# A two-layer decoder trunk: where the norms' squares are summed, and which engine splits one block of key weights

## The chip, the cores and the metric

One core of a Trainium2 chip runs the kernel. The metric is the device time of one execution in microseconds (us). The engines are TensorE (PE, the matmuls), VectorE (DVE), ScalarE (ACT), GpSimd (POOL), and SyncE (SP), whose queue issues the weight DMAs.

## What is computed

A trunk of two pre-norm residual layers on x of shape (1, 256, 1024), float32: an attention mixer, then a gated FFN with a causal depthwise convolution of width 3, and a last norm at the end. The first layer's mixer has two kinds of heads (one with a top-k selection), the second layer's a mixture of three dilated windows. Cut to what matters here:

```
def rmsnorm(x, g):
    y = x32 * lax.rsqrt(jnp.mean(x32 * x32, axis=-1, keepdims=True) + RMS_EPS)
    return (y * g.astype(jnp.float32)).astype(x.dtype)
...
def conv_ffn(h, w_up, conv_w, conv_b, w_down):
    u = h @ w_up
    ...
    val, gate = jnp.split(c, 2, axis=-1)
    return (jax.nn.silu(gate) * val) @ w_down
...
    for layer in range(DEPTH):
        h = rmsnorm(x, attn_norm[layer])
        ...
        x = x + mixed @ w_o[layer]
        h = rmsnorm(x, ffn_norm[layer])
        x = x + conv_ffn(h, w_up[layer], conv_w[layer], conv_b[layer], w_down[layer])
    return rmsnorm(x, final_norm)
```

## The kernel before

**Precision and weights.** Every large product is three matmuls, high x high, high x low and low x high (`mm3`, L125). An operand is split into a high part, which ACT copies into a rounded format (L121), and a low part, which DVE makes by subtraction (L122). Weights come in tiles of 1 MB by SP's queue (`load_cols` L90, `load_rows` L98). The tiles of the up projection and of q, k, v share three raw slots; five slots each hold the high and low parts. A load into a raw slot is issued when the last split that reads the slot's old contents is done. Names read as f0 (first FFN), f1 (second FFN), n1 (the norm ahead of the second layer's attention), q10, k10, v10 (first column block of that attention's projections), a0, a1 (the two attentions). f0w3_1h is the high part of the second weight block (the gate half, from the raw tile ug2) of up tile f=3; f0w3_0h is that of the value half (from uv2). Two consecutive f share a pair of raw tiles: uv0, ug0 serve f=0 and 1, uv2, ug2 serve f=2 and 3, uv4, ug4 serve f=4 and 5.

**The norms.** The residual x is kept transposed as xT, 8 blocks of 128 features by 256 tokens, and the products are formed from x times gain; the factor 1/sqrt(mean square) of each token is applied later, where a product leaves PSUM. `Norm.take` (L214) is called for each of four PSUM accumulators b: DVE adds it to xT (L219), ACT squares the result (L227), ACT and DVE make high and low parts, xh and xl (L203, L204). POOL adds the squares up as they come (L229, L231, L233: two of 128x512, three of 128x256 in each norm). After b = 3 PE sums over partitions ("sp", L239), DVE makes the mean ("v", L176), POOL the power -1/2 ("r", L178), DVE splits it and puts it on diagonals ("rh", "rl", "d", L183 to L190), PE broadcasts it to a row ("bp", L191), and ACT copies the row to SBUF ("b", L194). The sums and the broadcast use the PSUM bank called av.

**The FFN.** `ffn` (L470) runs over 22 tiles f. An up tile is 48 matmuls. Its PSUM banks rotate, `rot = [lg_tile, pt_tile, lg_tile, av_tile]`, so that f=3 is the first to use the bank av. DVE multiplies the tile by the scale row (us, L516), ACT and DVE do the convolution and the gate, ACT and DVE split the gated tile (g, L530 and L533), and three tiles later PE does its down product into the four accumulators f0o0 to f0o3. At the end of the first FFN the last tile's down products (g21) feed `take` of n1.

**The order.** No engine reorders at run time: each runs its own list. The list is set when the kernel is built, by a scheduler that simulates a timeline and takes, on each engine, what is ready and of the highest priority. The code narrows it: `tc.high_priority()` raises what stands in it, `keep_in_program_order` pins, and `issue_after(i)` (in `behind`, L107) keeps an instruction behind i. `n1.gate` are the last xh and xl of n1; weights split behind them don't come in their way. In the second attention (L751) the first half of the first key weights is split ahead of that gate, its low part on POOL:

```
        gate, low = (n1.gate, nc.gpsimd) if c == 0 else (None, nc.vector)
        proj_fm(wo1, 256 * c, n1.xh, n1.xl, q_evac(qs, rb1, f"q1{c}t"), f"q1{c}")
        proj_fm(wo1, 1024 + 256 * c, n1.xh, n1.xl, k_evac(ks, kl, rb1, f"k1{c}t"), f"k1{c}",
                (None, gate), (low, nc.vector))
```

Of the kernel before, what the change touches and what calls it, by code (L numbers as in the profile page):

```python
# [34 lines left out]
def trunk(ctx, tc, x, w_in_even, idx_k_norm, w_in_odd, w_o, rel_bias, attn_norm, ffn_norm,  # L35
          w_up, conv_w, conv_b, w_down, final_norm, c_onehot, out):
    nc = tc.nc
    cp = ctx.enter_context(tc.tile_pool(name="cp", bufs=1))
    wp = ctx.enter_context(tc.tile_pool(name="wp", bufs=2))
    tp = ctx.enter_context(tc.tile_pool(name="tp", bufs=2))  # L40
# [7 lines left out]
    def lg_tile(name):  # L48
        return pb.tile([P, 512], F32, tag="lg", name=name, bufs=2)
# [21 lines left out]
    ones = cp.tile([P, P], F32, tag="ones", name="ones")  # L71
# [39 lines left out]
                es.enter_context(tc.issue_after(i.ins))  # L111
            yield

    def split(view, shape, name, gate=None, low=nc.vector):
        with behind(gate):
            return split_now(view, shape, name, low)

    def split_now(view, shape, name, low):
        h = wp.tile([P] + shape, F32R, tag="wh", name=name + "h", bufs=5)
        l = wp.tile([P] + shape, F32R, tag="wl", name=name + "l", bufs=5)  # L120
        nc.scalar.activation(h, view, AF.Copy)  # L121
        low.tensor_tensor(l, view, h.bitcast(F32), ALU.subtract)  # L122
        return h, l

    def mm3(ps, wh, wl, ah, al, start, stop, swap=False, pin=False, **kw):  # L125
# [75 lines left out]
    def split_x(xh, xl, grow, k):  # L201
        g = gT[:, grow + k:grow + k + 1]
        a = nc.scalar.activation(xh[:, k, :], xT[:, k, :], AF.Copy, scale=g)  # L203
        v = nc.vector.scalar_tensor_tensor(xl[:, k, :], xT[:, k, :], g, xh[:, k, :].bitcast(F32),  # L204
                                           op0=ALU.mult, op1=ALU.subtract)
        return a, v

    class Norm:


        def __init__(self, grow, name):
            self.grow, self.name = grow, name

        def take(self, b, acc):  # L214
            if b == 0:
                self.xh, self.xl = norm_tiles(self.name)
            xv = xT[:, 2 * b:2 * b + 2, :]
            for i in range(2):
                nc.vector.tensor_tensor(xv[:, i, :], acc[:, i * S:(i + 1) * S], xv[:, i, :], ALU.add)  # L219
            with tc.high_priority():  # L220
                self.measure(b, xv)
            for k in (2 * b, 2 * b + 1):
                self.gate = split_x(self.xh, self.xl, self.grow, k)

        def measure(self, b, xv):
            sq = tp.tile([P, 2, S], F32, tag=("c", "c", "u", "c")[b], name=f"{self.name}sq{b}", bufs=(3, 3, 2, 3)[b])
            nc.scalar.activation(sq, xv, AF.Square)  # L227
            if b in (1, 2):
                nc.gpsimd.tensor_tensor(sq, sq, self.sq, ALU.add)  # L229
            if b >= 2:  # L230
                nc.gpsimd.tensor_tensor(sq[:, 0, :], sq[:, 0, :], sq[:, 1, :], ALU.add)  # L231
            if b == 3:
                nc.gpsimd.tensor_tensor(sq[:, 0, :], sq[:, 0, :], self.sq[:, 0, :], ALU.add)  # L233
            self.sq = sq
            if b < 3:
                return
            ps = av_tile(self.name + "sp")
            for t in range(2):
                nc.tensor.matmul(ps[:, t:t + 1], sq[:, 0, t * P:(t + 1) * P], ones[:, 0:1], start=True, stop=True)  # L239
            self.r = rsqrt_mean(ps[:, 0:2], D, self.name)  # L240
            self.rb = row_bcast(self.r, self.name)


    pin = tc.keep_in_program_order
    we = w_in_even[0]
    kiw_raw = cp.tile([P, 8, 80], F32, tag="kT", name="kiw_raw")
    nc.sync.dma_start(kiw_raw, we[:, 4096:4176].rearrange("(k p) c -> p k c", p=P))
# [18 lines left out]
    for b in range(4):  # L266
        h, l = (w[:, 2 * (b % 2):2 * (b % 2) + 2, :] for w in qi0_hl[b // 2])
# [6 lines left out]
        if b > 0:  # L274
            high = pin(nc.scalar.activation(h, wv, AF.Copy))
# [11 lines left out]

    def proj_fm(w2d, c0, xh, xl, evac, name, gate=(None, None), low=(nc.vector, nc.vector)):  # L290
        raw = load_cols(w2d, c0, name)
        ps = acc_tile(f"{name}p")
        for i in range(2):
            h, l = split(raw[:, :, i * P:(i + 1) * P], [8, P], f"{name}_{i}", gate[i], low[i])
            for k in range(KT):
                m = mm3(ps[:, i * S:(i + 1) * S], h[:, k, :], l[:, k, :], xh[:, k, :], xl[:, k, :],
                    k == 0 and i == 0, k == KT - 1, skip_group_check=True)
        evac(ps.rearrange("p (i c) -> p i c", i=2))
        return m
# [170 lines left out]
    def ffn(layer, norm, name, nxt, also=None):  # L470
        xh, xl = norm.xh, norm.xl
# [34 lines left out]
        for f in range(NF):  # L506
            if f % 2 == 0:
                raws = (load_cols(w_up[layer], f * P, f"{name}uv{f}"),
                        load_cols(w_up[layer], DFF + f * P, f"{name}ug{f}"))
            else:  # L510
                raw_dn = load_rows(w_down[layer], (f - 1) * P, f"{name}dn{f}", ("qT", "kT", "V")[f // 2 % 3])
                for i in range(2):
                    dn.append(raw_dn[:, i, :])
            ps = up(f, raws)
            u = tp.tile([P, 2, S], F32, tag="u", name=f"{name}us{f}")
            nc.vector.tensor_tensor(u, ps.rearrange("p (i c) -> p i c", i=2), rbb, ALU.mult)  # L516
            c = tp.tile([P, 2, S], F32, tag="c", name=f"{name}c{f}", bufs=3)
            for i in (1, 0):
                col = layer * 44 + i * NF + f
                nc.scalar.activation(c[:, i, :], u[:, i, :], AF.Identity, bias=cv[:, 3, col:col + 1],  # L520
                                     scale=cv[:, 2, col:col + 1])
                for j, sh in ((1, 1), (0, 2)):
                    nc.vector.scalar_tensor_tensor(c[:, i, sh:S], u[:, i, 0:S - sh], cv[:, j, col:col + 1],  # L523
                                                   c[:, i, sh:S], op0=ALU.mult, op1=ALU.add)
            sg = tp.tile([P, S], F32, tag="sg", name=f"{name}sg{f}")
            nc.scalar.activation(sg, c[:, 1, :], AF.Silu)
            nc.vector.tensor_tensor(sg, sg, c[:, 0, :], ALU.mult)
            g2 = tp.tile([P, 2, S], F32R, tag="g2", name=f"{name}g{f}", bufs=LAG + 2)
            gh, gl = g2[:, 0, :], g2[:, 1, :]
            high = nc.scalar.activation(gh, sg, AF.Copy)  # L530
            if also is not None:
                also(f, high.ins)
            nc.vector.tensor_tensor(gl, sg, gh.bitcast(F32), ALU.subtract)  # L533
            pend.append((f, gh, gl))
            if len(pend) > LAG:
                down(*pend.pop(0), dn.pop(0))
            if f == 1 and last:
                xtok = cp.tile([P, 2, D], F32, tag="qi", name=f"{name}xtok")
                for t in range(2):
                    for k4 in range(2):  # L540
                        px = acc_tile(f"{name}xt{t}{k4}")
                        for k in range(4):
                            nc.tensor.transpose(px[:, k * P:(k + 1) * P], xT[:, 4 * k4 + k, t * P:(t + 1) * P], ident)
                        nc.vector.tensor_copy(xtok[:, t, k4 * 512:(k4 + 1) * 512], px)
        if not last:
            down(*pend.pop(0), dn.pop(0))
        hl = [split(dn.pop(0), [D], f"{name}d{p[0]}") for p in pend]
        if not last:
# [205 lines left out]
    V, mxh, mxl = attn_tiles("a1")  # L754
    for c in range(4):
        qs, ks, kl = qk_tiles(c, "a1")
        gate, low = (n1.gate, nc.gpsimd) if c == 0 else (None, nc.vector)
        proj_fm(wo1, 256 * c, n1.xh, n1.xl, q_evac(qs, rb1, f"q1{c}t"), f"q1{c}")
        proj_fm(wo1, 1024 + 256 * c, n1.xh, n1.xl, k_evac(ks, kl, rb1, f"k1{c}t"), f"k1{c}",
                (None, gate), (low, nc.vector))  # L760
        proj_v(wo1, 2048 + 256 * c, n1.xh, n1.xl, r1, 256 * c, f"v1{c}", gate)
        for hp in (2 * c, 2 * c + 1):
            head_pair(hp, qs, ks, kl, lambda h: (nb1[:, h, P:S], nb1[:, h, :]), "a1")
# [45 lines left out]
```

## Time and profile before

| | us |
|---|---|
| median of 3 runs | 663.67 (663.56 to 664.44) |
| the profiled execution | 663.93 |
| its span on the core | 662.1 |
| PE busy | 649.3 (98%) |
| DVE busy | 530.5 (80%) |
| ACT busy | 406.2 (61%) |
| POOL busy | 58.0 (9%) |

The span runs from the first instruction to the last one on the core; the execution is 1.8 us longer. A share of busy time is a mean over stages: the first FFN runs from about 160 to 350 us of the span, the second layer's attention from there to 467, the second FFN to the end. Matmuls overlap, so the durations of single ones add up to more than the time in which they run; the distance of two starts tells what one costs.

### The profile page before, as it was taken

The numbers are of one execution on the slowest core, as the hardware profiler recorded it, in microseconds if no ns is written. First come the engines' busy times: TensorE is split into PE (matmuls) and PEld (weight loads), VectorE is DVE, ScalarE is ACT, GpSimd is POOL, SyncE is SP. The second block draws the span as 40 slices with busy tenths as digits, with TensorE's granted clock in tenths as the row PEclk, the third lists the DMA queues.
The fourth block names the chain that finished last, engine by engine and source line by source line (L and its number), as shares of the span: only waits on it lengthen the run. The fifth ranks groups of instructions, "written<-read, shape, count | busy, mean of one in ns | idle before, by whom it ended". The sixth has DMA issues, their size and how long they took to land.

```text
span 662.1 us, 12930 instructions
## 1 busy us (share of the span) xinstructions
PE 649.3 (98%) x5145; PEld 616.6 (93%) x5145; DVE 530.5 (80%) x1012; ACT 406.2 (61%) x710; POOL 58.0 (9%) x68
## 2 busy tenths in 40 slices
PE   8999999999999999999999999999999999999995
PEld 6999998988999999999989988999999999999994
DVE  5999998966898777777779977765999777777774
ACT  6766774765676555555546866764587555555553
POOL 0100001712100000000013111010300000000002
PEclk9999999999999999999999999999999999999998
DMA  9986644462766666666323534537366555555201
GB/s 272 292 243 188 174 137 153 157 220 98 247 216 207 208 207 207 207 207 207 128 65 128 192 101 155 191 128 256 117 184 227 195 186 185 184 185 187 105 1 63
DMA packets 91604, 116.01 MB, mean 175 GB/s; under 512 B 3447, under 2 KB 83191, under 8 KB 91544
## 3 DMA queue, kind: packets, MB, share of 16 engines
q1 hardware_dynamic: 86492, 110.09, 50.5%
q10 hardware_dynamic: 5052, 5.10, 3.3%
q8 instruction: 40, 0.66, 0.4%
q14 instruction: 20, 0.16, 0.1%
HBM read 113.35 MB, written 1.84 MB: 174 GB/s over the span
## 4 chain that ended last, share of the span: by engine, by line
PE 95%; DVE 2%; DMA 1%; issue 1%; SPq 0%; ACT 0%; POOL 0%; POOLq 0%; DVEq 0%
PE f0u L130 18%; PE f1u L130 18%; PE f1o L130 9%; PE f0o L130 9%; PE a0o L130 3%; PE a1o L130 3%; PE a0av L392 1%; PE a1av L392 1%; PE a_0pt L385 1%; PE v02p L130 1%; PE v11p L130 1%; PE v01p L130 1%; PE v12p L130 1%; PE v03p L130 1%; PE v13p L130 1%; PE k02p L130 1%
## 5 line engine op out<-in xcount | busy, mean ns | idle before, releaser
L130 PE MATMUL f0u<-f0xl,f0w_0h 128*128 128x256 f32 x176 | 49.5, 281 | 1.2 <-DVE f0xl L204 1.2
L130 PE MATMUL f1u<-f1xl,f1w_0h 128*128 128x256 f32 x176 | 49.5, 281 | 0.3
L130 PE MATMUL f0u<-f0xh,f0w_0l 128*128 128x256 f32 x176 | 49.2, 280 | 0.0
L130 PE MATMUL f1u<-f1xh,f1w_1h 128*128 128x256 f32 x176 | 49.2, 280 | 0.0
L130 PE MATMUL f0u<-f0xh,f0w_1l 128*128 128x256 f32 x176 | 49.1, 279 | 0.0
L130 PE MATMUL f1u<-f1xl,f1w_1h 128*128 128x256 f32 x176 | 49.1, 279 | 0.0
L130 PE MATMUL f1u<-f1xh,f1w_0l 128*128 128x256 f32 x176 | 49.1, 279 | 0.0
L130 PE MATMUL f0u<-f0xh,f0w_1h 128*128 128x256 f32 x176 | 49.1, 279 | 0.0
L130 PE MATMUL f0u<-f0xh,f0w_0h 128*128 128x256 f32 x176 | 49.1, 279 | 0.0
L130 PE MATMUL f0u<-f0xl,f0w_1h 128*128 128x256 f32 x176 | 49.1, 279 | 0.0
L130 PE MATMUL f1u<-f1xh,f1w_1l 128*128 128x256 f32 x176 | 49.1, 279 | 0.0
L130 PE MATMUL f1u<-f1xh,f1w_0h 128*128 128x256 f32 x176 | 49.1, 279 | 0.0
L523 DVE SCALAR_TENSOR_TENSOR f1c<-f1us,cv,f1c 128x255 f32<-128x255 f32 (+1 forms) x88 | 37.0, 475 | 0.7 <-ACT f1c L520 0.7
L523 DVE SCALAR_TENSOR_TENSOR f0c<-f0us,cv,f0c 128x255 f32<-128x255 f32 (+1 forms) x88 | 36.9, 476 | 0.0
L121 ACT ACTIVATE f1w_0h<-f1uv 128x1024 fp32r<-128x1024 f32 x22 | 23.2, 1056 | 21.9 <-PE f1u L130 21.9
L121 ACT ACTIVATE f0w_0h<-f0uv 128x1024 fp32r<-128x1024 f32 x22 | 23.3, 1057 | 21.8 <-PE f0u L130 21.5
L130 PEld LDWEIGHTS f0u<-f0xl,f0w_0h 128*128 128x128 f32 x176 | 33.1, 188 | 1.8 <-DVE f0xl L204 1.6
L130 PEld LDWEIGHTS f1u<-f1xl,f1w_0h 128*128 128x128 f32 x176 | 33.1, 188 | 1.6 <-DVE f1xl L204 0.8
L121 ACT ACTIVATE f0w_1h<-f0ug 128x1024 fp32r<-128x1024 f32 x22 | 23.3, 1059 | 17.4 <-PE f0o L130 12.2
L130 PEld LDWEIGHTS f1u<-f1xh,f1w_0h 128*128 128x128 f32 x176 | 33.1, 188 | 0.8
L130 PEld LDWEIGHTS f1u<-f1xh,f1w_0l 128*128 128x128 f32 x176 | 33.1, 188 | 0.0
L130 PEld LDWEIGHTS f1u<-f1xl,f1w_1h 128*128 128x128 f32 x176 | 33.1, 188 | 0.0
(1055 smaller groups left out, 2493.6 us busy)
## 6 DMA issues: line engine op xcount, KB each, us to landing
f0dn<-in_w_down_dram SPq DMA_DIRECT2D x11, 1024.0 KB, 5.0
f0uv<-in_w_up_dram SPq DMA_DIRECT2D x11, 1024.0 KB, 5.9
f0ug<-in_w_up_dram SPq DMA_DIRECT2D x11, 1024.0 KB, 5.0
f1dn<-in_w_down_dram SPq DMA_DIRECT2D x11, 1024.0 KB, 4.8
f1uv<-in_w_up_dram SPq DMA_DIRECT2D x11, 1024.0 KB, 6.7
f1ug<-in_w_up_dram SPq DMA_DIRECT2D x11, 1024.0 KB, 5.1
q<-in_w_in_even_dram SPq DMA_DIRECT2D x4, 1024.0 KB, 6.7
k<-in_w_in_even_dram SPq DMA_DIRECT2D x4, 1024.0 KB, 6.0
```

The source lines that it names most:

```text
L121: nc.scalar.activation(h, view, AF.Copy)
L130: m = nc.tensor.matmul(ps, w, a, start=start and i == 0, stop=stop and i == 2, **kw)
L385: nc.tensor.transpose(pt[:, c * P:(c + 1) * P], pr[:, c * P:(c + 1) * P], ident)
L392: nc.tensor.matmul(o[:, 0:S], V[:, 0, vc], pts[s][:, 0:S], start=True, stop=False)
L523: nc.vector.scalar_tensor_tensor(c[:, i, sh:S], u[:, i, 0:S - sh], cv[:, j, col:col + 1], c[:, i, sh:S], op0=ALU.mult, op1=ALU.add)
```

## The change

There are two. (1) In the norms f0, n1 and f1 the squares are kept until all four are there, and DVE sums them in four instructions (three of 128x512, one of 128x256), which may not stand ahead of the norm's last low part; before, POOL summed them in five. (2) The low part of the first half of the second layer's first key weights, k10_0l, is made by DVE instead of POOL, and its split may not stand ahead of the split of the last gated tile of the first FFN, g21. The parameter `low` goes, `split_now` is folded into `split`, and the line that defines `pin` moves up, with no effect on what runs. No load is added or removed.

```
         def take(self, b, acc):
...
+            sq = tp.tile([P, 2, S], F32, tag=("c", "c", "u", "c")[b], name=f"{self.name}sq{b}", bufs=(3, 3, 2, 3)[b])
             with tc.high_priority():
-                self.measure(b, xv)
+                nc.scalar.activation(sq, xv, AF.Square)
+            self.sq.append(sq)
             for k in (2 * b, 2 * b + 1):
                 self.gate = split_x(self.xh, self.xl, self.grow, k)
-
-        def measure(self, b, xv):
-            sq = tp.tile([P, 2, S], F32, tag=("c", "c", "u", "c")[b], name=f"{self.name}sq{b}", bufs=(3, 3, 2, 3)[b])
-            nc.scalar.activation(sq, xv, AF.Square)
-            if b in (1, 2):
-                nc.gpsimd.tensor_tensor(sq, sq, self.sq, ALU.add)
-            if b >= 2:
-                nc.gpsimd.tensor_tensor(sq[:, 0, :], sq[:, 0, :], sq[:, 1, :], ALU.add)
             if b == 3:
-                nc.gpsimd.tensor_tensor(sq[:, 0, :], sq[:, 0, :], self.sq[:, 0, :], ALU.add)
-            self.sq = sq
-            if b < 3:
-                return
+                with tc.high_priority():
+                    self.measure()
+
+        def measure(self):
+
+            a, b, c, d = self.sq
+            with tc.issue_after(self.gate[1].ins):
+                nc.vector.tensor_tensor(a, a, b, ALU.add)
+                nc.vector.tensor_tensor(c, c, d, ALU.add)
+                nc.vector.tensor_tensor(a, a, c, ALU.add)
+                nc.vector.tensor_tensor(a[:, 0, :], a[:, 0, :], a[:, 1, :], ALU.add)
             ps = av_tile(self.name + "sp")
...
-            nc.vector.tensor_tensor(gl, sg, gh.bitcast(F32), ALU.subtract)
+            low = nc.vector.tensor_tensor(gl, sg, gh.bitcast(F32), ALU.subtract)
...
         if not last:
+            nxt.behind = (high, low)
             down(*pend.pop(0), dn.pop(0))
...
-        gate, low = (n1.gate, nc.gpsimd) if c == 0 else (None, nc.vector)
+        gate, early = (n1.gate, n1.behind) if c == 0 else (None, None)
...
-                (None, gate), (low, nc.vector))
+                (early, gate))
```

The scheduler answers with another order around these places. On ACT at the start of the first FFN, from the second tile pair's last split on, before:

```order
L121 ACTIVATE f0w3_0h_2482<-f0uv2_2402 128x1024
L121 ACTIVATE f0w3_1h_2486<-f0ug2_2404 128x1024
L194 ACTIVATE f0b_2245<-f0bp_2238 128x256
L121 ACTIVATE f0d0h_2557<-f0dn1_2328 128x1024
L520 ACTIVATE f0c0_2315<-f0us0_2313,cv_683 128x256 x2
L121 ACTIVATE f0w4_0h_2590<-f0uv4_2585 128x1024
L520 ACTIVATE f0c1_2389<-f0us1_2387,cv_683 128x256 x2
L121 ACTIVATE f0w4_1h_2594<-f0ug4_2587 128x1024
```

and of after:

```order
L118 ACTIVATE f0w3_0h_2481<-f0uv2_2401 128x1024
L118 ACTIVATE f0w3_1h_2485<-f0ug2_2403 128x1024
L118 ACTIVATE f0d0h_2556<-f0dn1_2327 128x1024
L118 ACTIVATE f0w4_0h_2589<-f0uv4_2584 128x1024
L118 ACTIVATE f0w4_1h_2593<-f0ug4_2586 128x1024
L192 ACTIVATE f0b_2248<-f0bp_2241 128x256
```

The copy of the scale row, f0b, has moved from ahead of the splits d0h, w4_0h and w4_1h to behind them. On DVE in the same stretch, from the last low parts of the norm on, before:

```order
L204 SCALAR_TENSOR_TENSOR f0xl_2138<-xT_116,gT_113,f0xh_2137 128x256 x4
L122 TENSOR_TENSOR f0w1_0l_2332<-f0uv0_2252,f0w1_0h_2331 128x1024
L122 TENSOR_TENSOR f0w1_1l_2336<-f0ug0_2254,f0w1_1h_2335 128x1024
L122 TENSOR_TENSOR f0w2_0l_2408<-f0uv2_2402,f0w2_0h_2407 128x1024
L176 TENSOR_SCALAR f0v_2229<-f0sp_2226 128x2
```

and of after:

```order
L202 SCALAR_TENSOR_TENSOR f0xl_2138<-xT_116,gT_113,f0xh_2137 128x256 x4
L232 TENSOR_TENSOR f0sq0_2141<-f0sq0_2141,f0sq1_2167 128x512
L233 TENSOR_TENSOR f0sq2_2193<-f0sq2_2193,f0sq3_2219 128x512
L119 TENSOR_TENSOR f0w1_0l_2331<-f0uv0_2251,f0w1_0h_2330 128x1024
L234 TENSOR_TENSOR f0sq0_2141<-f0sq0_2141,f0sq2_2193 128x512
L119 TENSOR_TENSOR f0w1_1l_2335<-f0ug0_2253,f0w1_1h_2334 128x1024
L119 TENSOR_TENSOR f0w2_0l_2407<-f0uv2_2401,f0w2_0h_2406 128x1024
L235 TENSOR_TENSOR f0sq0_2141<-f0sq0_2141 128x256
L119 TENSOR_TENSOR f0w2_1l_2411<-f0ug2_2403,f0w2_1h_2410 128x1024
L174 TENSOR_SCALAR f0v_2232<-f0sp_2229 128x2
L119 TENSOR_TENSOR f0w3_0l_2482<-f0uv2_2401,f0w3_0h_2481 128x1024
```

The four sums stand among the weight splits, and the mean f0v has moved behind w2_1l. On PE the broadcast f0bp stood inside the tile f=1 (f0u1); now both its matmuls stand between the tiles f=2 and f=3, of after:

```order
L127 MATMUL f0u2_2405<-f0xh_2137,f0w2_1l_2411 128x256
L189 MATMUL f0bp_2241<-f0d_2240,ones_r_92 128x256 x2
L127 MATMUL f0u3_2480<-f0xh_2137,f0w3_0h_2481 128x256
```

The partition sums f0sp moved by 44 matmuls, within f=1. The second FFN's row is moved in the same way on the three engines, and that of n1 by some 50 places on PE. On DVE at the end of the first FFN k10_0l has come in between g21's low part and the residual adds of n1, of after:

```order
L525 TENSOR_TENSOR f0sg21_4411<-f0sg21_4411,f0c21_4404 128x256
L531 TENSOR_TENSOR f0g21_4414<-f0sg21_4411,f0g21_4414 128x256
L119 TENSOR_TENSOR k10_0l_4661<-k10_4657,k10_0h_4660 128x1024
L217 TENSOR_TENSOR xT_116<-f0o0_2552,xT_116 128x256 x2
```

Before, it stood on POOL, ahead of the first sum of n1's squares; nothing else moved on DVE there.

## Rows read from the trace of the kernel before

**Rows 1.** Busy line of the page, whole span

```profile
PE 649.3 (98%) x5145; PEld 616.6 (93%) x5145; DVE 530.5 (80%) x1012; ACT 406.2 (61%) x710; POOL 58.0 (9%) x68
```

**Rows 2.** PE's waits, whole span: us in total, times, longest

```profile
PE f0o L130 <- DVE f0g L533: 1.5, 1, 1.5
...
PE f0u L130 <- DVE f0xl L204: 1.2, 2, 0.8
```

**Rows 3.** Timeline, PE, first and last matmuls: start, us, instruction [idle before <-releaser]

```profile
1.34 3.59 PE L87 MATMUL warm_ps<-warm 128*128 128x512 bf16 x8 [1.34 <-DVE warm L84]
...
654.27 0.63 PE L130 MATMUL f1o<-f1d21h,f1g 128*128 128x512 f32 x2
654.74 0.40 PE L130 MATMUL f1o<-f1d21l,f1g 128*128 128x512 f32 x1
```

**Rows 4.** Timeline, POOL and DVE, start of the first FFN

```profile
158.91 2.71 POOL L229 TENSOR_TENSOR f0sq<-f0sq,f0sq 128x512 f32<-128x512 f32 x2 [23.80 <-ACT f0sq L227]
...
158.01 0.47 DVE L204 SCALAR_TENSOR_TENSOR f0xl<-xT,gT,f0xh 128x256 fp32r<-128x256 f32 x1
...
159.21 2.69 DVE L204 SCALAR_TENSOR_TENSOR f0xl<-xT,gT,f0xh 128x256 fp32r<-128x256 f32 x2
161.82 0.74 DVE L219 TENSOR_TENSOR xT<-a0o,xT 128x256 f32<-128x256 f32 x2
162.49 2.14 DVE L204 SCALAR_TENSOR_TENSOR f0xl<-xT,gT,f0xh 128x256 fp32r<-128x256 f32 x4
```

**Rows 5.** Timeline, PE, first FFN's first tiles

```profile
159.63 0.28 PE L130 MATMUL f0u<-f0xh,f0w_0h 128*128 128x256 f32 x1
...
167.28 0.28 PE L130 MATMUL f0u<-f0xh,f0w_0h 128*128 128x256 f32 x1
...
179.19 0.28 PE L130 MATMUL f0u<-f0xh,f0w_0h 128*128 128x256 f32 x1
```

**Rows 6.** Timeline, DVE and PE, start of the second FFN

```profile
466.18 2.79 DVE L204 SCALAR_TENSOR_TENSOR f1xl<-xT,gT,f1xh 128x256 fp32r<-128x256 f32 x2
...
470.11 0.67 DVE L544 COPY f1xtok<-f1xt 128x512 f32<-128x512 f32 x1
...
473.57 1.21 DVE L122 TENSOR_TENSOR f1w_0l<-f1uv,f1w_0h 128x1024 fp32r<-128x1024 f32 x1
...
466.82 0.28 PE L130 MATMUL f1u<-f1xh,f1w_0h 128*128 128x256 f32 x1
...
473.67 0.28 PE L130 MATMUL f1u<-f1xh,f1w_0h 128*128 128x256 f32 x1
...
486.96 0.28 PE L130 MATMUL f1u<-f1xh,f1w_0h 128*128 128x256 f32 x1
```

**Rows 7.** Timeline, POOL, DVE and PE, end of the first FFN

```profile
342.81 2.36 POOL L122 TENSOR_TENSOR k_0l<-k,k_0h 128x1024 fp32r<-128x1024 f32 x1 [172.83 <-ACT k_0h L121]
...
343.07 2.38 DVE L533 TENSOR_TENSOR f0g<-f0sg,f0g 128x256 fp32r<-128x256 f32 x1 [1.54 <-ACT f0g L530]
...
343.69 0.28 PE L130 MATMUL f0o<-f0g,f0d21h 128*128 128x256 f32 x1
...
355.80 0.28 PE L130 MATMUL q10p<-n1xh,q_1h 128*128 128x256 f32 x1
```

**Rows 8.** Timeline, SP's queue and ACT, first FFN

```profile
166.35 0.37 SPq L94 DMA_DIRECT2D f0ug<-in_w_up_dram  x1
...
171.49 1.06 ACT L121 ACTIVATE f0w_1h<-f0ug 128x1024 fp32r<-128x1024 f32 x1 [4.95 <-DMA f0ug<-in_w_up_dram]
...
174.35 0.36 ACT L194 ACTIVATE f0b<-f0bp 128x256 f32<-128x256 f32 x1
...
180.11 1.06 ACT L121 ACTIVATE f0w_1h<-f0ug 128x1024 fp32r<-128x1024 f32 x1 [0.30 <-DMA f0ug<-in_w_up_dram]
```

**Rows 9.** Windows: us, PE busy (x), PEld, DVE, ACT, POOL, PEclk, DMA share, GB/s

```profile
372.00:445.00 73.00, 73.00 (x589) 67.17 (x588) 55.09 (x147) 50.53 (x117) 6.61 (x6) 1.00 0.45 154
...
658.00:659.00 1.00, 0.00 (x0) 0.00 (x0) 0.35 (x1) 0.32 (x1) 0.00 (x0) 0.75 0.68 262
```

More of the change, by code (lines that the diff above doesn't have):

```diff
@@ L112, in behind, with split @@
             yield
-    def split(view, shape, name, gate=None, low=nc.vector):
+    def split(view, shape, name, gate=None):
         with behind(gate):
[L116 to L122, printed above, removed]
+            h = wp.tile([P] + shape, F32R, tag="wh", name=name + "h", bufs=5)
+            l = wp.tile([P] + shape, F32R, tag="wl", name=name + "l", bufs=5)
+            nc.scalar.activation(h, view, AF.Copy)
+            nc.vector.tensor_tensor(l, view, h.bitcast(F32), ALU.subtract)
         return h, l
@@ L133, in mm3 @@
         return m.ins
+    pin = tc.keep_in_program_order
     gps = lg_tile("gps")
@@ L211, in __init__ @@
         def __init__(self, grow, name):
-            self.grow, self.name = grow, name
+            self.grow, self.name, self.sq = grow, name, []
         def take(self, b, acc):
@@ L219, in take @@
                 nc.vector.tensor_tensor(xv[:, i, :], acc[:, i * S:(i + 1) * S], xv[:, i, :], ALU.add)
+            sq = tp.tile([P, 2, S], F32, tag=("c", "c", "u", "c")[b], name=f"{self.name}sq{b}", bufs=(3, 3, 2, 3)[b])
             with tc.high_priority():
-                self.measure(b, xv)
+                nc.scalar.activation(sq, xv, AF.Square)
+            self.sq.append(sq)
             for k in (2 * b, 2 * b + 1):
                 self.gate = split_x(self.xh, self.xl, self.grow, k)
-        def measure(self, b, xv):
-            sq = tp.tile([P, 2, S], F32, tag=("c", "c", "u", "c")[b], name=f"{self.name}sq{b}", bufs=(3, 3, 2, 3)[b])
-            nc.scalar.activation(sq, xv, AF.Square)
-            if b in (1, 2):
-                nc.gpsimd.tensor_tensor(sq, sq, self.sq, ALU.add)
-            if b >= 2:
-                nc.gpsimd.tensor_tensor(sq[:, 0, :], sq[:, 0, :], sq[:, 1, :], ALU.add)
-            if b == 3:
-                nc.gpsimd.tensor_tensor(sq[:, 0, :], sq[:, 0, :], self.sq[:, 0, :], ALU.add)
-            self.sq = sq
-            if b < 3:
-                return
+            if b == 3:
+                with tc.high_priority():
[7 more added lines that the diff above has]
+                nc.vector.tensor_tensor(a[:, 0, :], a[:, 0, :], a[:, 1, :], ALU.add)
             ps = av_tile(self.name + "sp")
             for t in range(2):
-                nc.tensor.matmul(ps[:, t:t + 1], sq[:, 0, t * P:(t + 1) * P], ones[:, 0:1], start=True, stop=True)
+                nc.tensor.matmul(ps[:, t:t + 1], a[:, 0, t * P:(t + 1) * P], ones[:, 0:1], start=True, stop=True)
             self.r = rsqrt_mean(ps[:, 0:2], D, self.name)
             self.rb = row_bcast(self.r, self.name)
-    pin = tc.keep_in_program_order
     we = w_in_even[0]
@@ L286, in trunk, with proj_fm @@
                                          start=n + k + i == 0, stop=n == 2 and k == KT - 1, skip_group_check=True))
-    def proj_fm(w2d, c0, xh, xl, evac, name, gate=(None, None), low=(nc.vector, nc.vector)):
+    def proj_fm(w2d, c0, xh, xl, evac, name, gate=(None, None)):
         raw = load_cols(w2d, c0, name)
@@ L293, in proj_fm @@
         for i in range(2):
-            h, l = split(raw[:, :, i * P:(i + 1) * P], [8, P], f"{name}_{i}", gate[i], low[i])
+            h, l = split(raw[:, :, i * P:(i + 1) * P], [8, P], f"{name}_{i}", gate[i])
             for k in range(KT):
```

## The prediction, made before the change was run

> **What bounds the kernel now.** I read the busy line of the page first, then PE's waits, then the timeline of the few places where PE waits, engine by engine. PE is busy 649.3 of the 662.1 us of the span [rows 1], so a change can give back at most the few waits that PE has, and can cost whatever new waits it makes. Two of these waits name what the change touches [rows 2]: 1.5 us once for a DVE low part at the end of the first FFN (g21), 1.2 us in two pieces for DVE low parts at the start of that FFN. DVE, ACT and POOL have time to spare as averages; what counts is when a few of their instructions end. PE issues a 128x512 matmul every 0.235 us at full clock, two in 0.47 [rows 3], so I take 0.117 us for a 128x256 one and 5.6 us for the 48 of an up tile.
>
> **The change part by part: what it gives.** *The squares leave POOL.* At the start of the first FFN DVE makes a low part of the norm's input in 0.47 us when POOL is quiet, and a pair of them took 2.69 us, from 159.21 to 161.90; POOL's two sums of squares ran from 158.91 to 161.62 [rows 4]. Nearly the whole stretch of the DVE pair lies inside those sums, and ends with them. [...] PE starts the tile f=0 at 159.63 and f=1 at 167.28 [rows 5], 7.65 us for 48 matmuls that need 5.6. With DVE undisturbed f=1 starts at about 165.25: **2.0 us gained**. At the start of the second FFN the same pair took 2.79 us. PE goes from 466.82 to 473.67 through 36 matmuls and 16 transposes [rows 6]; 36 x 0.117 + 16 x 0.095 (an estimate, from what they take where they run on) = 5.7, against 6.85: **1.1 us gained**.
>
> *The key weights leave POOL.* POOL's subtraction ran from 342.81 to 345.17 and g21's low part on DVE from 343.07 to 345.45 [rows 7], although such a 128x256 instruction is no larger than those of 0.47 us. PE had issued the first matmul of g21 at 343.69 and had to wait. From there to the second half of q10 PE has 76 matmuls, 8.9 us, so 352.6 instead of 355.80 [rows 7]: **3.2 us gained**, 1.7 of it the g21 wait, the rest waits for the n1 low parts and their slower neighbours, as in the first FFN. The subtraction now costs DVE 1.2 us (the 128x1024 low part of 1.21 us [rows 6]) between g21's low part, which ends at 343.5, and the first residual add. It ends at about 344.7. The first two accumulator pieces that the adds need leave PE at about 344.6, so it is hidden; if that cover were gone it would cost up to 1.2.
>
> *The four sums on DVE.* Three of 128x512 at half the 1.21 us and one of 128x256 at 0.3 make 2.1 us per norm. Two stand directly behind the last low part, the other two among weight splits. They release POOL's earlier end but make the scale row later, which is the cost below. The first layer's norm n0 is not touched, and no DMA is added.
>
> **What it costs.** The scheduler has put the scale row's copy f0b on ACT behind the highs of w4, as the rows of the order show, and its broadcast on PE directly ahead of tile f=3, which uses the same PSUM bank and so can't start before f0b is done. In the trace of before f0b ran at 174.35 and f=3 began at 179.19 [rows 5, 8] with nothing to wait for. Now ACT comes to f0b only after w4_1h, which waits for the DMA ug4, and that DMA is issued when the raw slot of uv2 comes free, behind the low part w3_0l; w3_0l stands on DVE behind w2_1l and f0v, and w2_1l needs the DMA ug2, issued behind w1_0l. Step by step from the end of w1_0l: DMA 5.14 (issued at 166.35, its split begins at 171.49 [rows 8]), ACT split 1.06, DVE low part 1.21, f0v 0.1, w3_0l 1.15, DMA 5.14 again, ACT split 1.06, f0b 0.36: 15.2 us, with the hand-overs 15.3. That these splits wait for their DMAs in before too is seen at 180.11, where ACT is released by ug4 [rows 8].
>
> First FFN: behind 159.21 DVE has two low parts, two adds (0.74 the pair), four low parts, two sums, w1_0l. The four low parts took 2.14 us with some of POOL in them [rows 4], and I take 0.44 each: 0.9 + 0.75 + 1.8 + 1.2 + 1.2 = 5.85, so w1_0l ends at 165.0, f=3 can start at 180.3. PE, 2.0 us earlier than before, is there at 177.2: a wait of some 3.1 us that takes the 2.0 back and **1.1 us more**.
>
> Second FFN: behind 466.18 [rows 6] six low parts (2.6), two adds (0.75), four PSUM copies (0.67 in the row, which counts the overlap with the next; 0.6 each, 2.4), two sums (1.2), w1_0l (1.2): 8.15, so w1_0l ends at 474.3, where before it was 474.78. The gain is small because the sums come into the same stretch. f=3 starts at 489.6, before it was 486.96 [rows 6]: **2.6 us lost**, the 1.1 gained included.
>
> Norm n1's scale row is late as well, 42 matmuls or some 5 us later on PE. There the row is wanted by the evacuation of q10 and k10, and the first logits come after more than 50 matmuls of other work. Between 372 and 445 PE has no idle time at all [rows 9], so the attention behind has cover; I put 0.1 us on it, from nothing to 2.
>
> Sum: first FFN +1.1, n1 -3.2, second FFN +2.6, cover +0.1: +0.6 us. I set it on the median, 663.67, since the profiled execution (663.93) lies only 0.26 above it: 664.3. The two ends of the unknown terms: each DMA of the two chains 0.3 less or more (four x 0.3), DVE's stretch 0.3 either way in each FFN: about 1.5 either way if most go together.
>
> **The rivals.** *A, the clock falls in the new wait (slower).* In the second FFN PE would stand still for some 3.7 us ahead of f=3 (485.9 to 489.6), broken only by the second broadcast matmul. [...] The price: the eight warm-up matmuls at the start took 3.59 us, at full clock they'd have taken 1.9, so 1.7 us: 666.0. It decides if the rows around 489 show a granted clock below 1.00; the broadcast in the wait, and the waits of before, after which the clock stayed at 1.00, speak against. [...] Chance 0.10.
>
> *B, the second layer's attention loses its cover (slower).* With the row of n1 some 5 us later, the query and key evacuations of the first four heads bunch up on DVE and ACT behind the splits of v10. If the first logits then wait, 1 to 2 us are lost: about 665.8. For it: DVE gets 1.2 + 2.1 us more in that stretch. Against it: no PE wait there in before. Chance 0.12.
>
> *C, the new wait doesn't come (faster).* Should ug4 land early enough, or f0b run when its input is there, only the gains are left: -2.0 -3.2 -1.1 = -6.3, 657.4; with the wait in one FFN alone, 660.5 (the first) or 661.1. For it: nothing in the arithmetic needs f0b that late. Against: engines run their instructions in order, and every step of the chain has its row. Chance 0.11.
>
> *D, the collision isn't POOL's (slower, the change doesn't do what it says).* If the low parts are slow for another reason, the gains of 2.0 and 1.1 fall away and the sums come on top: w1_0l 1.2 later than before in both, f=3 at 182.8 and 491.3, so +3.6 and +4.3, n1 at best -1.7: about 670. The coincidence of ends in [rows 4, 7] speaks against. Chance 0.03.
>
> **How the numbers follow.** Forecast 664.3, chance 0.64, its own range 662.8 to 665.8. About 0.2% (1.33 us) is what a measurement of this kernel can tell from no change, so "same" is 662.34 to 665.0. Of the 0.64 I put 0.47 inside, 0.14 above and 0.03 below. With B half inside (0.06), A, D and the rest of B above (0.19) and C below (0.11): faster 0.14, same 0.53, slower 0.33. The range 662.5 to 666.2 takes in the forecast, A and most of B, and leaves out C and D.
>
> **What would show it.** DVE low parts of the norms at 0.47 us or a little less, g21's at 0.42 to 0.5; PE without the waits of [rows 2]; f=1 of the first FFN 5.6 us behind f=0 instead of 7.65. Then two new PE waits for ACT's f0b and f1b, of about 3 and 3.7 us, ahead of f=3, with ACT's w4_1h just before, released by the DMA ug4. If these waits are missing or below 1 us, the sum is wrong by that much, towards C. If they are there but PE's distance from f=3 to the end differs from before, look at A in the clock and at B in the waits of the logits.

## The result: 4.5 us slower, and the profile after

The changed kernel takes 668.58 us (667.31 to 670.14, 4 runs) beside 664.06 (663.56 to 664.67) for the kernel before: a ratio of 1.0073, with a 95% interval of 1.0056 to 1.0091. In a second set of runs it took 667.36 beside 663.93, ratio 1.0053 (1.0037 to 1.0068). The forecast was 664.3 in a range of 662.5 to 666.2: the single effects had the sign and nearly the size that was forecast, but the time lies above the range.

The page's busy line of the changed kernel, which answers to [rows 1]:

```profile
PE 653.4 (98%) x5145; PEld 620.9 (93%) x5145; DVE 528.1 (79%) x1025; ACT 406.2 (61%) x710; POOL 41.3 (6%) x52
```

POOL has 16 instructions less. PE has as many as before and is 4.1 us longer busy, though it computes the same: a first sign that something slows PE while it works. The waits of PE over the whole span (us in total, times, longest), beside [rows 2]:

```profile
PE f1u L127 <- ACT f1b L192: 1.9, 1, 1.9
PE f0u L127 <- ACT f0b L192: 1.9, 1, 1.9
...
PE f1bp L189 <- DVE f1d L188: 1.1, 1, 1.1
...
PE f0bp L189 <- DVE f0d L188: 0.5, 1, 0.5
```

Both waits of [rows 2] are gone. In their place PE waits ahead of f=3 in both FFNs, in two pieces: for DVE's second diagonal ahead of the second broadcast matmul, then for ACT's copy of the scale row. That is 2.4 us in the first FFN and 3.0 in the second.

**First FFN.** The timelines of DVE, SP's queue, ACT and PE of the changed kernel (start, us, instruction [idle before <-releaser]), beside [rows 4], [rows 5] and [rows 8]:

```profile
160.38 0.87 DVE L202 SCALAR_TENSOR_TENSOR f0xl<-xT,gT,f0xh 128x256 fp32r<-128x256 f32 x2
...
164.69 1.22 DVE L119 TENSOR_TENSOR f0w_0l<-f0uv,f0w_0h 128x1024 fp32r<-128x1024 f32 x1
```

```profile
174.77 0.37 SPq L94 DMA_DIRECT2D f0ug<-in_w_up_dram  x1
```

```profile
180.00 1.06 ACT L118 ACTIVATE f0w_1h<-f0ug 128x1024 fp32r<-128x1024 f32 x1 [3.32 <-DMA f0ug<-in_w_up_dram]
180.97 0.36 ACT L192 ACTIVATE f0b<-f0bp 128x256 f32<-128x256 f32 x1
```

```profile
160.81 0.28 PE L127 MATMUL f0u<-f0xh,f0w_0h 128*128 128x256 f32 x1
...
179.13 0.38 PE L189 MATMUL f0bp<-f0d,ones_r 128*128 128x256 f32 x1 [0.50 <-DVE f0d L188]
181.39 0.58 PE L127 MATMUL f0u<-f0xh,f0w_0h 128*128 128x256 f32 x1 [1.88 <-ACT f0b L192]
181.77 0.42 PE L127 MATMUL f0u<-f0xl,f0w_0h 128*128 128x256 f32 x1
181.98 0.41 PE L127 MATMUL f0u<-f0xh,f0w_0l 128*128 128x256 f32 x1
```

The pair of low parts takes 0.87 us where it took 2.69. Then the chain of the prediction runs off: ug4 is issued at 174.77, ACT has stood 3.32 us for it when it splits it at 180.00, the copy f0b follows at 180.97, and f=3 starts at 181.39, 20.58 us behind f=0 (19.56 before). And the matmuls behind it start 0.21 us apart instead of 0.117. The windows of this stretch and of the same place in the second FFN (window, us, PE busy (x), PEclk, DMA share, GB/s) say why:

```profile
180.00:185.00 5.00, 3.61 (x18) 0.66 0.52 175
...
490.00:495.00 5.00, 3.95 (x21) 0.68 0.43 145
```

The granted clock has a mean of 0.66 and 0.68 in these windows. In slices of 0.2 us it reads 0.50 from 181.2 to 184.4 and from 491.8 to 495.0, and 1.00 ahead of and behind these stretches, but for the slices at their edges: it fell to half for some 3.4 us in each FFN. In the second FFN PE had even started f=3 at full pace when its matmuls went from 0.12 to 0.2 us apart:

```profile
491.62 0.29 PE L127 MATMUL f1u<-f1xl,f1w_0h 128*128 128x256 f32 x1
491.74 0.39 PE L127 MATMUL f1u<-f1xh,f1w_0l 128*128 128x256 f32 x1
491.93 0.42 PE L127 MATMUL f1u<-f1xh,f1w_0h 128*128 128x256 f32 x1
```

**Between the FFNs.** DVE and PE of the changed kernel, beside [rows 7]:

```profile
345.75 0.43 DVE L531 TENSOR_TENSOR f0g<-f0sg,f0g 128x256 fp32r<-128x256 f32 x1 [0.48 <-ACT f0g L528]
346.70 1.22 DVE L119 TENSOR_TENSOR k_0l<-k,k_0h 128x1024 fp32r<-128x1024 f32 x1 [0.52 <-ACT k_0h L118]
```

```profile
347.43 0.40 PE L127 MATMUL f0o<-f0g,f0d21h 128*128 128x256 f32 x2
...
356.29 0.28 PE L127 MATMUL q10p<-n1xh,q_1h 128*128 128x256 f32 x1
```

g21's low part takes 0.43 us (2.38 before), k_0l is hidden behind PE's down products, and from g21 to q10's second half PE needs 8.86 us where it needed 12.11.

**Second FFN**, beside [rows 6]:

```profile
468.22 0.28 PE L127 MATMUL f1u<-f1xh,f1w_0h 128*128 128x256 f32 x1
...
491.05 0.38 PE L127 MATMUL f1u<-f1xh,f1w_0h 128*128 128x256 f32 x1 [1.91 <-ACT f1b L192]
```

```profile
474.43 1.22 DVE L119 TENSOR_TENSOR f1w_0l<-f1uv,f1w_0h 128x1024 fp32r<-128x1024 f32 x1
```

f=3 starts 22.83 us behind f=0, before it was 20.14.

All kernels of this study, cut at five starts on PE that each of them has (first matmul of f0, first of g21, q10's second half, first of f1, last matmul), in us:

| | f0 to g21 | g21 to q10 | q10 to f1 | f1 to last |
|---|---|---|---|---|
| before | 184.06 | 12.11 | 111.02 | 187.92 |
| changed | 186.62 | 8.86 | 111.93 | 192.26 |
| changed, second profile | 185.34 | 8.87 | 111.97 | 192.46 |
| fill | 185.23 | 8.87 | 111.97 | 192.88 |
| fill_again | 185.12 | 8.87 | 111.98 | 192.84 |
| sums_only | 186.76 | 10.67 | 112.01 | 192.48 |
| k10_only | 184.04 | 10.45 | 111.06 | 187.96 |
| row_early | 184.55 | 8.95 | 112.00 | 188.10 |
| diag_early | 182.21 | 8.86 | 111.99 | 187.79 |
| n1_early | 182.31 | 8.87 | 112.95 | 187.93 |
| n1_mid | 182.29 | 8.87 | 112.52 | 187.79 |

The differences of the first two rows are +2.56, -3.25, +0.91 and +4.34, together +4.56, close to the 4.5 of the medians. The two profiled executions (669.53 and 663.93) lie 5.6 apart, because f0 itself begins at 160.81 in this profile and at 159.63 in that of before; in the second profile of the changed kernel it begins at 159.05. This offset stands within the first 20 us already and comes from no edit.

### The profile page after: what moved, and what is told of

Read it like the earlier page. It is cut to its first block, busy times and chain, and to the rows that moved or that the text cites. A ratio compares the mean times of both kernels' runs of the same rounds, so it can differ in the third digit from the quotient of the medians.

```text
span 667.7 us, 12909 instructions
## 1 busy us (share of the span) xinstructions
PE 653.4 (98%) x5145; PEld 620.9 (93%) x5145; DVE 528.1 (79%) x1025; ACT 406.2 (61%) x710; POOL 41.3 (6%) x52
## 4 chain that ended last, share of the span: by engine, by line
PE 90%; DMA 4%; DVE 3%; ACT 1%; issue 0%; SPq 0%; POOL 0%; POOLq 0%; ACTq 0%; DVEq 0%
PE f1u L127 16%; PE f0u L127 16%; PE f0o L127 9%; PE f1o L127 9%; PE a0o L127 3%; PE a1o L127 3%; DMA f0ug<-in_w_up_dram 2%; DMA f1ug<-in_w_up_dram 2%; PE a1av L390 1%; PE a0av L390 1%; PE a_0pt L383 1%; PE v02p L127 1%; DMA xtok<-in_x_dram 1%; PE v13p L127 1%; PE v01p L127 1%; PE q13p L127 1%
## 5 line engine op out<-in xcount | busy, mean ns | idle before, releaser
L521 DVE SCALAR_TENSOR_TENSOR f1c<-f1us,cv,f1c 128x254 f32<-128x254 f32 (+1 forms) x88 | 37.2, 478 | 0.8 <-ACT f1c L518 0.7
L521 DVE SCALAR_TENSOR_TENSOR f0c<-f0us,cv,f0c 128x254 f32<-128x254 f32 (+1 forms) x88 | 37.2, 480 | 0.1
L127 PEld LDWEIGHTS f0u<-f0xh,f0w_0h 128*128 128x128 f32 x176 | 33.8, 192 | 2.1 <-ACT f0b L192 2.1
L118 ACT ACTIVATE f1w_1h<-f1ug 128x1024 fp32r<-128x1024 f32 x22 | 23.3, 1061 | 19.9 <-DMA f1ug<-in_w_up_dram 10.3
L118 ACT ACTIVATE f0w_1h<-f0ug 128x1024 fp32r<-128x1024 f32 x22 | 23.3, 1060 | 19.4 <-PE f0o L127 10.4
```

Source lines behind the costliest of these rows:

```text
L127: m = nc.tensor.matmul(ps, w, a, start=start and i == 0, stop=stop and i == 2, **kw)
```

## The experiments

**Each half of the change alone.** *k10_only* is the kernel before with

```
-        gate, low = (n1.gate, nc.gpsimd) if c == 0 else (None, nc.vector)
+        gate, early = (n1.gate, n1.behind) if c == 0 else (None, None)
...
-                (None, gate), (low, nc.vector))
+                (early, gate))
```

> The second half of the change alone: k10_0l made by DVE behind g21, the squares still summed by POOL as before. Theory 1: g21's low part at 0.43 us and no wait of PE for it, 1.7 us gained; the n1 low parts still collide with POOL's sums, so 1.5 us of the 3.2 stay; nothing moves in the two FFNs, no late row, and the second attention takes the 111.0 us of before from q10's second half to f1: 663.6 - 1.7 = 661.9. Theory 2: k10_0l delays the residual adds by its 1.2 us: 663 or more.

Measured 662.13 us (661.72 to 663.19) beside 663.93, ratio 0.9971 (0.9960 to 0.9982). The wait of [rows 2] for g21 is gone, those for the norms' low parts are still there, and g21's low part is back at its length; waits of PE and timeline of DVE:

```profile
PE f0u L130 <- DVE f0xl L204: 1.2, 2, 0.8
PE q10p L130 <- DVE n1xl L204: 0.8, 2, 0.5
```

```profile
342.87 0.42 DVE L533 TENSOR_TENSOR f0g<-f0sg,f0g 128x256 fp32r<-128x256 f32 x1 [0.48 <-ACT f0g L530]
```

So this half is a gain by itself, 1.8 us by the medians and 1.66 in g21 to q10 (10.45 for 12.11), the only place that changes.

*sums_only* is the changed kernel with k10_0l on POOL again:

```
-                (early, gate))
+                (None, gate), (low, nc.vector))
```

> The first half of the change alone: the norms' squares summed by DVE, but k10_0l still made by POOL. Theory 1: both waits for the scale row and both clock falls as in the changed kernel, and in addition the wait of PE for g21's low part, 1.7 us, which is the part of k10_0l: 670.3. The n1 low parts run at 0.47 us, since the squares are off POOL. Theory 2: the n1 gain of 3.2 us came from the squares alone: 668.6, as the changed kernel.

Measured 670.90 us (670.02 to 672.59) beside 663.60, ratio 1.0105 (1.0088 to 1.0122). PE waits and two DVE rows:

```profile
PE f1u L127 <- ACT f1b L192: 2.1, 1, 2.1
PE f0u L127 <- ACT f0b L192: 1.9, 1, 1.9
PE f0o L127 <- DVE f0g L531: 1.5, 1, 1.5
```

```profile
345.06 2.39 DVE L531 TENSOR_TENSOR f0g<-f0sg,f0g 128x256 fp32r<-128x256 f32 x1 [1.56 <-ACT f0g L528]
...
351.57 0.48 DVE L202 SCALAR_TENSOR_TENSOR n1xl<-xT,gT,n1xh 128x256 fp32r<-128x256 f32 x1
```

With POOL's subtraction back, g21's low part is at 2.39 us again and the wait of 1.5 is there, while the n1 low parts, whose sums have left POOL, stay at 0.48. The two collisions are separate: 1.66 us belong to k10_0l, 1.44 to the squares, and 3.25 came from both. The loss is all in the half that moves the squares.

That the time comes near the 670.3 expected is in part luck. In this profile the clock fell in the second FFN alone (its mean over the execution is 0.996, as in the changed kernel's second profile, and f1 to last takes 192.48 us beside 192.46 there), and f0 to g21 is as long as in the changed kernel for another reason (last section). Of its five runs the profiled one and one more have a mean granted clock of 0.996, the other three 0.989: in those the clock was low for longer than in the profile, and where is not known.

**The position of the row's copy.** *row_early* is the changed kernel with the splits of w4 kept behind the copy (`rb_copy` is the ACT instruction of L192):

```
-                    norm.gate if 1 <= f < 4 else None) for i in range(2)]
+                    norm.gate if 1 <= f < 4 else (norm.rb_copy,) if f == 4 else None) for i in range(2)]
```

> The changed kernel with one constraint more: the splits of the up weights w4 may not stand ahead of the copy of the scale row (f0b, f1b) on ACT. Theory 1: the copy then waits for its broadcast only and no longer for the DMA ug4. f=3 starts about 18.4 us behind f=0 in the first FFN (20.6 in the changed kernel) and 19.9 in the second (22.8); PE waits below 1 us each time, too short for the clock, which stays at 1.00. The time falls by 2.2 + 1.6 + 2.9 + 1.7 = 8.4, to about 660. Theory 2: the position on ACT is not what holds the row; DVE's diagonals, behind w2_1l, or the PSUM bank hold it as long, and the waits stay over 1.5 us with the clock falling: 667 or more.

Measured 661.31 us (660.08 to 662.00) beside 663.60, ratio 0.9956 (0.9942 to 0.9971). ACT and PE in the first FFN:

```profile
176.51 0.38 ACT L192 ACTIVATE f0b<-f0bp 128x256 f32<-128x256 f32 x1 [3.82 <-PE f0bp L189]
```

```profile
176.08 0.40 PE L189 MATMUL f0bp<-f0d,ones_r 128*128 128x256 f32 x2
176.95 0.39 PE L127 MATMUL f0u<-f0xh,f0w_0h 128*128 128x256 f32 x1 [0.47 <-ACT f0b L192]
```

ACT now waits for the broadcast, not for a DMA, PE waits 0.47 us, its matmuls go on 0.12 us apart behind it, and the mean granted clock is 0.998 (0.993 to 0.996 in the runs of the changed kernel). f=3 starts 18.38 us behind f=0, as expected. The time was expected at 660; in the profiled execution (661.15) the rest is that f0 to g21 came out at 184.55, 1.6 longer than its waits explain (last section).

*diag_early* adds that the split of w2_1 may not stand ahead of DVE's last diagonal of the row:

```
+                    (norm.diag,) if (f, i) == (2, 1) else norm.gate if 1 <= f < 4 else (norm.rb_copy,) if f == 4 else None)
```

> As the version in which w4 may not stand ahead of the row's copy, and besides the split of w2_1 may not stand ahead of DVE's last diagonal of the scale row, so that the mean of squares doesn't wait on DVE behind a weight block that is still in flight. Theory 1: no wait over 0.6 us ahead of f=3, all of the gain that the changed kernel makes elsewhere stays: 664.1 - 2.0 - 3.2 - 1.1 + 0.9 (lost in the second attention) = 658.7, with f=3 some 17.6 us behind f=0 in the first FFN. Theory 2: w2_1l delayed by the diagonals makes PE wait inside f=2: 660 or more.

Measured 659.09 us (658.94 to 660.63) beside 663.60, ratio 0.9930 (0.9915 to 0.9945): faster than both kernels. The two rows of PE's waits that lead its list:

```profile
PE warm_ps L87 <- DVE warm L84: 1.3, 1, 1.3
PE f1u L127 <- ACT f1b L192: 0.5, 1, 0.5
```

f0 to g21 takes 182.21, 1.85 less than before: the 2.0 us that the prediction put on the squares of the first FFN, no longer taken back. In the second FFN the squares gain 0.9 of the 1.1 us up to f=1, which starts 7.41 us behind f=0 where it was 8.69 with 0.36 of partition sums in between. But a wait of 0.5 for the row is left ahead of f=3, and f1 to last takes 187.79 beside 187.92, so hardly any of it stays. The wait for the row is the cause of the loss in the FFNs, and its place in the queues of ACT and DVE is the cause of the wait.

**The clock.** *after_again* is the changed kernel, unedited, *fill* and *fill_again* (the same kernel) have matmuls that nothing reads in the wait (`row_last` holds the two broadcast matmuls):

```
+            if f == 3:
+                fill = acc_tile(f"{name}fill")
+                first, second = row_last[-2:]
+                with tc.issue_after(first.ins):
+                    m = fill_run(fill, xh, 10 if last else 5)
+                with tc.issue_after(second.ins):
+                    m = fill_run(fill, xh, 18)
...
+                m = nc.tensor.matmul(fill[:, 0:S], ones_r, xh[:, 0, :], start=True, stop=True)
```

> The changed kernel with matmuls put into PE's wait ahead of the tile f=3 of both FFNs: 5 (first FFN) or 10 (second) between the two broadcast matmuls and 18 behind them, of ones times the first block of xh into a spare PSUM bank that nothing reads. No result changes, and f0b and f1b come no earlier. [...] With PE kept at work the granted clock stays at 1.00 through 180 to 195 and 480 to 500, f=3 starts where it did against the start of its FFN (20.6 and 22.8 us behind f=0), and the time falls by 3.3 us, to about 665.3. Theory 2: the clock rows only accompany the loss, which is made by the late scale row further down: the time stays within 1 us of 668.6.

> The changed kernel once more, unedited, to have it on the same chip beside the others. Theory 1: 4 to 5 us over before, waits of 2.4 to 3.0 us ahead of f=3 and the granted clock below 1.00 behind at least one of them; its times lie 1.5 us apart in steps, since a wait is followed by the fall in some executions and in others not. Theory 2, the loss has nothing to do with the clock: the same time with and without the fall in the profile.

> The version with matmuls in the wait once more, since in its first profile the DMA ug2 of the second FFN took 7.05 us, where 5.16 was seen in the changed kernel, and f=3 came 2.1 us later for it. Theory 1: no fall of the clock in either FFN; where that DMA takes 5.2 us again, 3.2 us below the changed kernel with two falls, 1.6 below it with one. Theory 2: within 0.5 us of the changed kernel.

Measured: fill 667.47 us (666.63 to 667.71) beside 663.60, after_again 667.36 (666.26 to 669.50) and fill_again 668.09 (666.83 to 668.83) beside 663.93. By their times filling brings nothing, and neither did after_again's times lie in steps of 1.5 us (666.26, 666.67, 666.92, 667.79, 668.80, 669.50) or 4 to 5 us over before. The profiles tell more. Windows behind the two waits, after_again first, then fill:

```profile
180.00:185.00 5.00, 5.00 (x44) 1.00 0.14 44
...
490.00:495.00 5.00, 5.00 (x34) 0.75 0.00 0
```

```profile
180.00:185.00 5.00, 5.00 (x45) 1.00 0.15 51
...
490.00:495.00 5.00, 4.98 (x42) 1.00 0.17 57
```

In the changed kernel's second profile PE waits as long in the first FFN (0.52 and 2.00 us) and the clock does not fall there; in the second FFN it falls again. The one kernel thus shows f0 to g21 with and without the fall, 186.62 and 185.34, and f=3 stands 20.58 and 20.73 us behind f=0: from f=3 on it is 166.04 beside 164.61, so a fall costs 1.4 us. With PE filled, the clock stays at 1.00 behind both waits (the windows of fill); over the whole of each run its mean is 0.996 to 0.999 in the twelve runs of fill, 0.993 to 0.996 in the ten of the changed kernel. From f=3 to the last matmul the second FFN takes 167.95 and 167.89 us, where the changed kernel takes 169.43 and 169.51 and the kernel before 167.78: a fall costs 1.6 us there.

Why the time doesn't show it: in both profiles of fill the split of ug2 in the second FFN begins 7.07 and 7.03 us behind its issue, not 5.16 (5.39 in the changed kernel's second profile). SP's queue and ACT of fill:

```profile
472.55 0.37 SPq L94 DMA_DIRECT2D f1ug<-in_w_up_dram  x1
```

```profile
479.62 1.06 ACT L118 ACTIVATE f1w_1h<-f1ug 128x1024 fp32r<-128x1024 f32 x1 [9.43 <-DMA f1ug<-in_w_up_dram]
```

so that f=3 starts 24.93 and 24.95 us behind f=0, 2.1 later than in the changed kernel, which eats the 1.6 that the clock gave. PE's and DVE's work up to that DMA stands at the same distances in both kernels. What differs is in the DMA queues between issue and split (packets, MB, share of 16 engines), fill first, then the changed kernel:

```profile
q1 hardware_dynamic: 1869, 1.90, 82.9%
q8 instruction: 1, 0.02, 1.8%
```

```profile
q1 hardware_dynamic: 1197, 1.21, 70.4%
```

In fill a packet of the queue that the profile calls instruction lies inside this load and takes some 2.0 us of one DMA engine (1.8% of 16 engines in 7.07 us); fill_again has it too, and neither profile of the changed kernel has it there. At a later load of the gate half the same is seen: 6.4 us to landing in both profiles of fill, with such a packet inside, and 5.2 in the changed kernel without. Where the packet comes late, 4.4 us behind the issue at 567.94 in the changed kernel, the load lands after 5.3 us all the same. That the added matmuls moved this packet into the load is therefore likely, but no run tests it. The price of the clock is read from the stretches, not from the medians of fill.

**The second attention.** In every kernel with the squares on DVE, q10 to f1 takes 111.9 to 112.0 us or more, in before and k10_only 111.0. *n1_early* and *n1_mid* are diag_early with n1's row brought forward, behind it v10's splits in the one, q11's in the other:

```
-        proj_v(wo1, 2048 + 256 * c, n1.xh, n1.xl, r1, 256 * c, f"v1{c}", gate)
+        proj_v(wo1, 2048 + 256 * c, n1.xh, n1.xl, r1, 256 * c, f"v1{c}", (n1.diag,) if c == 0 else None)
```

```
-        proj_fm(wo1, 256 * c, n1.xh, n1.xl, q_evac(qs, rb1, f"q1{c}t"), f"q1{c}")
+        proj_fm(wo1, 256 * c, n1.xh, n1.xl, q_evac(qs, rb1, f"q1{c}t"), f"q1{c}",
+                ((n1.diag,), (n1.diag,)) if c == 1 else (None, None))
```

> As the version with w2_1 behind the diagonals and w4 behind the row's copy, and besides v10's splits may not stand ahead of n1's last diagonal; n1's broadcast then stands 56 matmuls behind the start of q10's second half (before 58, changed kernel 106), the first logits 149 (127, 174). Theory 1: the 0.9 us that the second attention lost (111.0 to 111.9 us) come from the late row, and most of them come back: 658.3. Theory 2: they come from the other interleaving of small matmuls there: 659.1, as without this constraint.

> As the version with w2_1 behind the diagonals and w4 behind the row's copy, and besides q11's splits (instead of v10's) may not stand ahead of n1's last diagonal: n1's broadcast stands 78 matmuls behind the start of q10's second half (before 58, without this constraint 106), v10 is not held up. Theory 1: the late row alone makes the second attention longer: 111.0 to 111.5 us from q10's second half to f1, and 658.7. Theory 2: it is the order of the 48 transposes and 64 products with V on PE, which stays as in the changed kernel behind the first heads: 111.9 us again and 659.1.

Measured 660.83 us (660.32 to 661.53) beside 663.93, and 659.66 (659.47 to 660.04) beside 663.72. Both are longer than diag_early in this stretch, 112.95 and 112.52, so neither theory's time came. n1_early pays for v10 at once:

```profile
PE v10p L127 <- DVE v_0l L119: 0.7, 1, 0.7
...
PE n1bp L189 <- DVE n1d L188: 0.3, 1, 0.3
```

An earlier row did not bring the 0.9 back in the total, but it came with new costs, so the total can't say what its lateness is worth; the single products can. Summed from PE's timeline (each matmul to the start of the next), the 48 transposes of the probabilities take 4.0 us in before and in k10_only and 4.5 in the changed kernel, and the 64 products with V 10.4, 10.4 and 11.0, in stretches where no wait of PE is shown. The 0.9 is therefore in how these small matmuls are placed among the large ones, which the scheduler did otherwise once n1's row came later. In n1_early, whose row comes as early as before, the products with V are back at 10.4 and the transposes stay at 4.5; in n1_mid both are as in the changed kernel. So the transposes don't depend on the row, and for the products with V that stays open. The neighbours of the transposes can be read from the same timelines: from its start to that of the next matmul a transpose takes 0.03 us when a matmul of a projection or of the logits follows, 0.12 when another transpose does and 0.20 when a product with V does. Before has 20, 26 and 2 of these, the changed kernel 17, 27 and 4, which makes the 0.5.

## Why the prediction was wrong

**What held.** The low parts were slow for POOL's work beside them, as read: 2.69 to 0.87 us for the pair, 2.38 to 0.43 for g21, and each half of the change alone frees its own. Why POOL's work slows DVE's beside it no run tests. The n1 gain was put at 3.2 and is 3.25. The late row was put at f=3 1.1 us later in the first FFN and 2.6 in the second; it is 1.02 and 2.69. n1's broadcast was put 42 matmuls and some 5 us later, and is 48 and 5.6. From the end of w1_0l to f=3 it takes 15.5 us (165.91 to 181.39) and 15.4, for 15.3, with the two DMAs and the ACT splits as told. f=1 starts 5.83 us behind f=0, for 5.6. Cover of k10_0l: it lies under PE's down products, as told.

**What failed.** Two steps.

The first is that the sum took PE's new waits at their length alone, with nothing for slower matmuls behind them (0.21 us apart instead of 0.117, at a granted clock of 0.50); that was left to rival A. A was named for the second FFN, with the price of 1.7 us, an estimate from the eight warm-up matmuls, and given 0.10 because the broadcast matmul stands inside the wait and because the clock had stayed at 1.00 behind the waits of before. Those waits were of 1.5 us and less; the new ones are of 2.4 and 3.0. In the second FFN the clock fell in all three profiles of kernels that have the wait (both of the changed kernel and sums_only), in the first FFN, for which no fall was considered at all, in one of three (the first profile of the changed kernel). The broadcast matmul in the middle did not prevent it. The rows show the fall, with 0.66 and 0.68 granted in the two windows of the first profile and 0.75 in 490 to 495 of the second, and the first FFN of the second profile shows that the same wait can also pass without it (1.00 in 180 to 185). Behind PE's last matmul the clock of the kernel before falls too: it is 1.00 up to 658 us, 0.75 in the next us [rows 9] and 0.50 from 659 on. The price: 1.4 to 1.6 us each, so 1.6 to 3.0 in the sum that had nothing for it. No run shows the 1.7 of rival A: over the warm-up (1.34 to 4.93 us) the granted clock of the kernel before is 1.00. Nor does one show the 1.6 and 1.7 in the sum of row_early, or the 3.3 that fill was to bring, as the price of the two falls; these were the author's estimates, and the stretches showed 1.4 and 1.6.

The second is the term for the second attention's cover, put at 0.1 with bounds from nothing to 2; it is 0.9. The mechanism of rival B, first logits that wait, did not come: PE's waits show none there. It is the order of small matmuls, and it was priced by waits only.

With both the sum closes: +1.0 (first FFN) -3.25 +2.7 (second FFN) +0.9 (attention) make +1.4, and one to two falls of the clock make that 3.0 to 4.4; measured are +3.4 and +4.5 by the medians. So the mechanisms of the sum held, each within 0.1 us, and what was missing is these two terms.

Rivals C and D are out: the wait came in both FFNs, and the collision was POOL's.

## What to carry to other kernels

A change that takes work off a busy pair of engines is judged also by what a static scheduler then does with everything else: here some 5 us of real gains (1.85 and 3.25, by the table) were lost because the scheduler had put a small copy on ACT, and the few short DVE instructions ahead of it, behind splits whose weights were still in flight; two ordering constraints brought most of them back (659.09 beside 663.60). Where an engine runs its list in order, as ACT did here (it stood 3.32 us for ug4, the last 0.5 of them with the copy's input at hand: the second broadcast matmul ended at 179.51), look for a short instruction on the critical path behind one that waits for a DMA. And price a new wait of PE of 2 to 3 us at its length and, with its chance, the slower matmuls behind it (1.4 to 1.6 us in this kernel at a granted clock of 0.50, behind four of six such waits), not at its length alone.

## What the runs showed of the hardware that was not expected

The same wait on PE, 2.4 us at the same place of the same kernel, was followed by a fall of the granted clock in one profile and not in another. The times of the changed kernel spread over 3.2 us (666.26 to 669.50) where those of before beside them spread over 1.7, but that the falls make this spread is not shown: of the 2.6 us between its two profiled executions (669.53 and 666.92) 1.8 stood ahead of f0, and the fastest run (666.26) has a lower mean clock, 0.994, than the one of 666.92 (0.996).

Matmuls can run 0.9% slower for a whole stage with the granted clock at 1.00 throughout. Windows of the first FFN, where all kernels do the same work: fill first, then row_early.

```profile
200.00:340.00 140.00, 140.00 (x1202) 1.00 0.58 187
```

```profile
200.00:340.00 140.00, 140.00 (x1191) 1.00 0.59 187
```

Eleven matmuls fewer in 140 us. sums_only shows 1191 too, before 1202, the changed kernel 1203 in both profiles. Between f=3 and g21 this makes 166.17 us (row_early) and 166.18 (sums_only) where fill has 164.53, with no wait of PE shown in between; in the second FFN the same kernels run at the usual pace. From start to start PE's 128x256 matmuls have two paces, 116.7 and 117.8 ns. In sums_only the slower one begins behind the wait ahead of f=3; in row_early it begins some 7 us earlier, behind the four short matmuls of the partition sums (f0sp, at 169.74), and is at 117.9 ns from 173.84 to 176.08:

```profile
169.74 0.50 PE L238 MATMUL f0sp<-ones,f0sq 128*128 128x1 f32 x4
```

In the first profile of the changed kernel it is the other way round: ahead of f0sp (172.06) PE runs at the slower pace (117.8 ns from 166.5 to 171.9), behind it at the faster one (116.7 from 172.7 to 178.2). So this is no state of a whole execution, but one that PE enters and leaves within it. What sets it is open; it is as large as a fall of the clock and would be taken for one from the times alone.
